# Moving the memory operands, the output rows and three buffers in a fused hybrid-trunk layer

## The chip, the cores and the metric

The kernel runs on one core of a Trainium2 chip. The metric is device time in microseconds for one execution of the whole layer: lower is better. The engines are named as in the profile: PE is TensorE (PEld its weight loads), DVE is VectorE, ACT is ScalarE, POOL is GpSimd, SP is SyncE, which here only starts DMAs.

## The reference

The layer has three residual parts on a sequence of 1024 tokens with 1024 channels, all in float32. Only the first two are touched by the change.

```python
# 1. token mixing
h = rms_norm(x, mix_pre_g)
proj = h @ w_in                                   # u | q | k | v | forget gate
y_ssm = s5_mixer(u, ...)                          # diagonal state space, GELU, GLU
y_fox = forgetting_attention(q, k, v, f_logit)    # 8 causal heads of 64
y_mix = concatenate([rms_norm(y_ssm, ssm_out_g), rms_norm(y_fox, fox_out_g)], axis=-1)
x = x + rms_norm(y_mix @ w_out, mix_post_g)
# 2. cross-attention into 256 memory tokens, 4 heads of 256
h = rms_norm(x, xa_pre_g)
x = x + rms_norm(memory_cross_attention(h, mem_n, xa_wq, xa_wkv, xa_wo), xa_post_g)
# 3. SwiGLU feed-forward
x = x + rms_norm(swiglu(h, w_gate, w_up, w_down), ffn_post_g)
```

The end of `s5_mixer` is the gated linear unit, the GLU: `g = gelu(y); out = g * sigmoid(g @ glu_w + glu_b)`. `mem_n` is `rms_norm(mem, mem_g)`, and `kv = mem_n @ xa_wkv` gives keys and values of the memory.

## The kernel before

**Arithmetic.** Every large product is made of three: an operand is split into a high part that the matmul takes as is, and a low part that is the rest (`split`, lines 113 to 117: one ScalarE pass, then one VectorE pass). `mm3` (lines 122 to 124) issues high x high, high x low and low x high.

**Order.** The kernel is one straight program without loops on the chip. A planner orders the instructions of each engine before the program runs, from a model of their times: what stands earlier in the Python text (or in a `tc.high_priority` block) goes first among those that it holds to be ready, and an instruction which needs a buffer can be placed only when one is to be had. `tc.issue_after(ins)` queues what its block holds behind `ins`; `behind()` (line 694) is that with the newest entry of the list `last`, which holds ScalarE instructions: one Gelu of the state space output, then the exponential of every attention unit.

**Buffers.** All large tiles come from a few pools. `slab`: 16 buffers of 8 KB per partition, used by nearly all stages. `raw`: two buffers of 4 KB, the landing place of most weights (`load_w`, line 152). `whl`: three buffers for split weights. The pool `t4` has tags: a (2 buffers), b (2), c (3), d (1), e (1), t2 (3), yt (2). `load_w(..., stage="e")` lands a weight in a buffer of that tag instead of in `raw`.

**The stages around the change**, with the time at which they run in the profiled execution:

- `in_proj` (up to about 230 us): the input projection, with the state space model beside it. At its end `ssm_out` (line 634) makes the state space output in two halves `s_` of four PSUM banks each, `b` 0 to 3, each ended by a Gelu (line 645), turns it (line 655) and splits it into the slabs `gl`. Two of the eight v tiles of `v1` are left over for the next stage.
- Attention, `fox` (line 696; about 228 to 486 us). A unit is one head and one block of 128 tokens, 64 in all; `scores` runs two units ahead of `turn` (transposes of the probabilities, line 758) and `values` (line 772). A score bank is freed by the VectorE pass of line 737. `prepare(h)` loads a head's queries, keys and gates on SP; `load_v(c)` loads the values of four heads. `values` collects squares in a tile of tag d.
- `fillers` (line 975) are pieces of other work that `paced` deals out beside the attention units, 1.02 for each: the rest of `v1`, the eight pieces of `glu`, the first output rows, `mem_load` (the memory, normalised and split into two slabs, its VectorE multiply at line 959), the 16 tiles of `mem_tile` (keys and values of the memory, stored to kv_d), the remaining output rows, and the first half of `build_a` (query weights times memory keys).
- `out_ssm` (line 818) makes the output rows: the state space half of the output projection, scaled by `r_s` (line 836), stored to `t1_d` on POOL's queue (line 840; the profile calls it t_d). `r_s` comes from `glu_stats`, which sums the GLU's squares, collected in `acc` (tag d), over channels (line 237). Before, it stood inside `out_ssm`, after the first two rows.
- After attention the attention half of the output projection is added. Its weights `wo` are loaded and split (lines 1024 to 1029). Then comes one loop turn `n` for each 128 tokens (line 1033): a tile `t` (tag a or b) is loaded with the half result from `t1_d` (line 1039), the matmuls' result is added (line 1046), its square is summed (line 1048), it is scaled on POOL (line 1050) and added to x (line 1054). `build_a(1)` is stepped in between.
- Then the cross-attention's output weights are folded into the memory's values (`VW`, line 1208), with eight weights `a["wo"]`, two of them landed in tag e.

## Time and profile before

| what | value |
|---|---|
| three runs | 1410.9, 1415.4, 1419.39 us; median 1415.4 |
| profiled execution | 1412.18 us |
| its span, first to last instruction | 1410.4 us |
| mean granted clock of TensorE | 0.99 |
| DMA traffic | 239.45 MB, mean 170 GB/s |

The page cuts the span into 40 slices of 35.3 us. Its rows for TensorE and its clock read:

```profile
PE   9999999999999898999999999999999999999997
PEclk9999999889999999999999999999999999999999
```

A digit is the busy share in tenths, 9 meaning 90% or more. In the second row, a digit is the clock that was granted. Slices 8 and 9 (247 to 317 us) have a lower clock, and slices 14 and 16 (458 to 494 and 529 to 564 us) a lower share. What follows looks into those places with finer stretches.

### The profile page before, as it was taken

To read this page: it belongs to the slowest core of one execution; us is meant where nothing else is said; L and a number is where in the kernel's file an instruction comes from. 1 tells how busy PE (TensorE), PEld (TensorE's weight loads), DVE (VectorE), ACT (ScalarE), POOL (GpSimd) and SP (SyncE) were. 2 spreads that over 40 slices of the span, in tenths; PEclk is the share of its full clock that TensorE was granted. 3 is DMA by queue.
4 is the path that set the end of the run, shared out by engine and by line. 5 is a ranking of instruction groups with operands and counts; after the bars stand their busy time and mean duration, and the time that the engine had idled before them with its cause. 6 is when DMAs were issued, how large, how long until landed. Compare 5 with 4: busy or idle time off the path is not lost.

```text
span 1410.4 us, 20272 instructions
## 1 busy us (share of the span) xinstructions
PE 1381.5 (98%) x7353; PEld 1163.3 (82%) x7353; DVE 952.1 (68%) x1719; ACT 652.8 (46%) x1289; POOL 378.7 (27%) x430
## 2 busy tenths in 40 slices
PE   9999999999999898999999999999999999999997
PEld 7889888889888786888888788888888888888886
DVE  8949945857666687545467767777776676555566
ACT  7383345666566555433344532333333334544351
POOL 0011110011111133001021377676766651000021
PEclk9999999889999999999999999999999999999999
DMA  6335665357562855024467345554444447965544
GB/s 217 91 107 162 204 224 135 91 165 224 187 180 95 214 185 201 1 83 159 147 213 250 102 174 195 186 173 168 144 159 151 162 150 244 344 203 194 179 165 164
DMA packets 104502, 239.45 MB, mean 170 GB/s; under 512 B 11465, under 2 KB 40137, under 8 KB 104273
## 3 DMA queue, kind: packets, MB, share of 16 engines
q1 hardware_dynamic: 85872, 176.24, 39.8%
q0 software_dynamic: 18528, 61.91, 12.3%
q8 instruction: 58, 0.95, 0.3%
q14 instruction: 44, 0.35, 0.1%
HBM read 169.43 MB, written 77.33 MB: 175 GB/s over the span
## 4 chain that ended last, share of the span: by engine, by line
PE 60%; DVE 1%; ACT 0%; issue 0%; DVEq 0%; ACTq 0%
PE x L1281 17%; PE g L1281 13%; PE x L1544 7%; PE g L1544 7%; PE x L123 2%; PE x L124 2%; PE g L122 2%; PE x L122 2%; PE g L124 2%; PE g L123 2%; PE g L1066 1%; PE g L1177 1%; DVE c L1054 0%; DVE whl L115 0%; ACT yt L1048 0%
## 5 line engine op out<-in xcount | busy, mean ns | idle before, releaser
L1281 PE MATMUL x<-slab,op 128*128 128x512 f32 x984 | 233.2, 389 | 0.5 <-DVE op L115 0.5
L1281 PEld LDWEIGHTS x<-slab,op 128*128 128x128 f32 x984 | 184.7, 188 | 39.2 <-DVE op L115 1.0
L1281 PE MATMUL g<-slab,op 128*128 128x512 f32 x744 | 178.7, 389 | 0.0
L115 DVE TENSOR_TENSOR slab<-slab 128x1024 fp32r<-128x1024 f32 (+2 forms) x92 | 110.6, 1208 | 86.6 <-ACT slab L113 84.4
L1281 PEld LDWEIGHTS g<-slab,op 128*128 128x128 f32 x744 | 139.7, 188 | 29.0
L122 PE MATMUL g<-slab,whl 128*128 128x512 f32 (+1 forms) x416 | 151.7, 365 | 0.8 <-ACT slab L485 0.4
L124 PE MATMUL g<-slab,whl 128*128 128x512 f32 (+1 forms) x416 | 148.9, 359 | 0.0
L123 PE MATMUL g<-slab,whl 128*128 128x512 f32 (+1 forms) x416 | 148.3, 356 | 0.0
L113 ACT ACTIVATE slab<-slab 128x1024 fp32r<-128x1024 f32 (+2 forms) x92 | 94.9, 1036 | 107.9 <-DMA slab<-hs_d 79.0
L1544 PE MATMUL g<-slab 128*128 128x512 f32 x462 | 126.6, 389 | 0.0
L1544 PE MATMUL x<-slab 128*128 128x512 f32 x462 | 126.6, 389 | 0.0
L1544 PEld LDWEIGHTS g<-slab 128*128 128x128 f32 x462 | 86.7, 188 | 18.0
L1544 PEld LDWEIGHTS x<-slab 128*128 128x128 f32 x462 | 86.7, 188 | 18.0
L115 DVE TENSOR_TENSOR op<-slab,op 128x512 fp32r<-128x512 f32 x80 | 84.4, 1066 | 11.6 <-ACT op L113 11.3
L1357 POOL TENSOR_TENSOR wt<-wt 128x256 f32<-128x256 f32 x88 | 83.0, 943 | 21.3 <-DMA wt<-in_w_down 18.0
L122 PEld LDWEIGHTS g<-slab,whl 128*128 128x128 f32 x416 | 78.6, 189 | 12.0 <-ACT whl L113 0.6
L124 PEld LDWEIGHTS g<-slab,whl 128*128 128x128 f32 x416 | 78.4, 189 | 11.7 <-DVE whl L115 0.2
L122 PE MATMUL g<-whl,slab 128*128 128x256 f32 (+2 forms) x288 | 86.8, 310 | 1.2 <-ACT yt L318 0.7
L123 PEld LDWEIGHTS g<-slab,whl 128*128 128x128 f32 x416 | 78.6, 189 | 10.8
L113 ACT ACTIVATE op<-slab 128x512 fp32r<-128x512 f32 x80 | 50.0, 627 | 79.3 <-PE x L1281 38.0
L124 PE MATMUL g<-whl,slab 128*128 128x256 f32 (+2 forms) x288 | 85.9, 299 | 0.0
L123 PE MATMUL g<-whl,slab 128*128 128x256 f32 (+2 forms) x288 | 85.9, 298 | 0.0
(385 smaller groups left out, 2890.6 us busy)
## 6 DMA issues: line engine op xcount, KB each, us to landing
hs_d<-ev POOLq DMA_DIRECT2D x77, 256.0 KB, 2.6
slab<-hs_d SPq DMA_DIRECT2D x35, 512.0 KB
wt<-in_w_down SPq DMA_DIRECT2D x44, 256.0 KB
wt_d<-wt POOLq DMA_DIRECT2D x22, 512.0 KB, 5.1
slab<-in_w_gate SPq DMA_DIRECT2D x20, 512.0 KB
slab<-in_w_up SPq DMA_DIRECT2D x20, 512.0 KB
slab<-wt_d SPq DMA_DIRECT2D x20, 512.0 KB
wd_d<-in_w_down SPq DMA_DIRECT2D x33, 256.0 KB
```

The lines of the kernel that those rows point to most:

```text
L113: first = act.activation(out=hi, in_=src, func=AF.Copy, scale=1.0 if mul is None else mul)
L115: (lo_eng or dve).tensor_tensor(out=lo, in0=src, in1=hi.bitcast(F32), op=ALU.subtract)
L122: pe.matmul(ps, lh, rh, start=first, stop=False)
L123: pe.matmul(ps, lh, rl, start=False, stop=False)
L124: pe.matmul(ps, ll, rh, start=False, stop=last)
L1066: pe.transpose(tp[:, k], src[:, (k0 + k) * P:(k0 + k + 1) * P], ident)
L1177: turned = pe.transpose(tp[:, k], h3[:, (4 * n + k) * P:(4 * n + k + 1) * P], ident)
L1281: pe.matmul(ps, x[:, k], y[:, k], start=first and k + n == 0, stop=k == 3 and n == 2, skip_group_check=not first)
L1357: pool.tensor_tensor(out=o, in0=x, in1=y, op=ALU.subtract)
L1544: pe.matmul(banks[n][j], xo[:, u, js], wo[:, v], start=ends[0] and k == 0, stop=ends[1] and k == 2, skip_group_check=onto is not None)
```

## The change

The diff, whole but for unchanged lines:

```diff
 def ssm_out():
-                    if (s_, b) == (0, 3):
+                    if (s_, b) == (0, 0):
                         last.append(g_)
 def glu(ys):
-        acc = tt("d")
+        acc = tt("e")
 def prepare(h):
-            sp.dma_start(out=ncb, in_=nc_d[h:h + 1, :].broadcast_to([P, S]))
             heads[h] = (qs, ka, ncb)
             q, k = qs.bitcast(F32), ka.bitcast(F32)
-            for t in range(2):
-                sp.dma_start(out=q[t * 64:t * 64 + 64], in_=qk_d[h // 2, t, r0:r0 + 64])
-            for rr in (0, 64):
-                sp.dma_start(out=k[rr:rr + 64], in_=qk_d[4 + h // 2, :, r0:r0 + 64].rearrange("t p s -> p t s"))
+            with behind():
+                sp.dma_start(out=ncb, in_=nc_d[h:h + 1, :].broadcast_to([P, S]))
+                for t in range(2):
+                    sp.dma_start(out=q[t * 64:t * 64 + 64], in_=qk_d[h // 2, t, r0:r0 + 64])
+                for rr in (0, 64):
+                    sp.dma_start(out=k[rr:rr + 64], in_=qk_d[4 + h // 2, :, r0:r0 + 64].rearrange("t p s -> p t s"))
 def fox(yf):
         prepare(0)
-        load_v(0)
...
-                if (h, t) == (3, 5):
-                    load_v(1)
+                if (h, t) in ((0, 3), (3, 5)):
+                    load_v(h // 2)
 def out_ssm(ys):
-                made = []
                 for j in range(j0, j0 + 2):
...
-                    made.append((j, ps))
-                    if cc + j0 == 0:
-                        yield
-                        if j == 0:
-                            continue
-                        glu_stats()
-                    for jj, ps in made:
-                        act.activation(out=o[:, jj - j0], in_=ps, func=AF.Copy, scale=r_s[:, jj:jj + 1])
-                    made = []
+                    act.activation(out=o[:, j - j0], in_=ps, func=AF.Copy, scale=r_s[:, j:j + 1])
                     if j == j0:
                         yield
+    mem = []
+
+    def mem_load(r):
+        rb = row_bcast(r, 2)
+        mem.extend((slab([P, KT, 256]), slab([P, KT, 256])))
+        for k in range(0, KT, 4):
+            m = raw([P, 4, 256])
+            sp.dma_start(out=m, in_=a["memT"].rearrange("(k p) m -> p k m", p=P)[:, k:k + 4])
+            for kk in range(4):
+                dve.tensor_tensor(out=m[:, kk], in0=m[:, kk], in1=rb, op=ALU.mult)
+                split(mem[0][:, k + kk], mem[1][:, k + kk], m[:, kk], g_mem[:, k + kk:k + kk + 1])
 def in_proj():
         drain(go)
+        mem_load(r_mem[0])
-    def mem_load(r, out):
...
-                with behind():
-                    dve.tensor_tensor(out=m[:, kk], in0=m[:, kk], in1=rb, op=ALU.mult)
-                    split(mh[:, k + kk], ml[:, k + kk], m[:, kk], g_mem[:, k + kk:k + kk + 1])
-                if kk % 2:
-                    yield
-        out.extend((mh, ml))
 def fillers():
         yield from glu(ys)
-        mem = []
-        rows = out_ssm(ys)
-        step(rows)
-        yield
-        for _ in mem_load(r_mem[0], mem):
-            step(rows)
-            yield
         for i in range(16):
             mem_tile(i, *mem)
+            if i == 1:
+                glu_stats()
             yield
+        rows = out_ssm(ys)
         yield from rows
         yield from build_a(0)
 # after attention
     for i in range(4):
-        w = raw([P, D])
-        sp.dma_start(out=w, in_=a["w_out_f"][i])
+        if i % 2 == 0:
+            w = slab([P, 2, D], F32)
+        sp.dma_start(out=w[:, i % 2], in_=a["w_out_f"][i])
         hl = slab([P, 2, D])
-        split(hl[:, 0], hl[:, 1], w)
+        split(hl[:, 0], hl[:, 1], w[:, i % 2])
-        t = tt("aab"[n % 3])
+        t = tt("aabaabae"[n])
 # folding wo into the memory's values
-        wo_ = [load_w(a["wo"][2 * h + d], 512, stage="e" if (2 * h + d) % 3 == 2 else None) for d in range(2)]
+        wo_ = [load_w(a["wo"][2 * h + d], 512, stage={2: "a", 5: "e"}.get(2 * h + d)) for d in range(2)]
```

In words:

- The memory's operands are made at the end of `in_proj`, right behind `ssm_out`, in the order of the text and no longer behind an attention unit. Before, they were made in four pieces among the fillers after the GLU.
- `glu_stats` follows the second memory tile, and all output rows come after the sixteenth.
- The GLU's sum of squares `acc` lies in tag e instead of d.
- The loads of `prepare` stand in a `behind()` block, the list `last` begins with an earlier Gelu, and the first half of the values is loaded at unit (0, 3) instead of ahead of the loop.
- The attention half of the output projection's weights lands in two slabs instead of in `raw`.
- In the loop after attention, the last tile `t` (n = 7) has tag e instead of a. The third weight folded into the memory's values (number 2) lands in tag a instead of e; the sixth (number 5) stays in e.

## The prediction

> **What bounds the kernel now.** I read the page first (span, engines, chain), then tables of busy time by stretch, then the waits of TensorE, then the timeline of the stretches in which it has gaps.

> ```profile
> span 1410.4 us, 20272 instructions
> PE 1381.5 (98%) x7353; PEld 1163.3 (82%) x7353; DVE 952.1 (68%) x1719; ACT 652.8 (46%) x1289; POOL 378.7 (27%) x430
> ```

> TensorE has something in flight for all but 28.9 us. The diff adds or drops no matmul, so it can only win TensorE's gaps and the time in which its clock is held down. The table by stretch (columns: stretch and length, then busy time of PE, PEld, DVE, ACT, POOL, then granted clock, DMA share, GB/s) shows where these lie in the part that the diff touches:

> ```profile
> 270.30:273.30 3.00, 1.04 (x11) 0.63 (x10) 3.00 (x9) 2.97 (x6) 0.00 (x0) 0.94 0.00 0
> 273.30:290.00 16.70, 14.20 (x59) 11.95 (x61) 11.29 (x27) 11.33 (x26) 1.31 (x2) 0.50 0.47 133
> 464.00:493.00 29.00, 24.81 (x176) 19.77 (x175) 16.72 (x28) 14.61 (x28) 2.85 (x3) 1.00 0.83 221
> 535.00:537.00 2.00, 1.08 (x5) 0.80 (x5) 1.77 (x7) 1.41 (x6) 1.41 (x1) 1.00 0.65 203
> 547.10:552.90 5.80, 3.46 (x13) 1.91 (x11) 3.07 (x6) 2.34 (x11) 2.19 (x2) 0.99 0.28 93
> 552.90:559.50 6.60, 5.33 (x12) 3.77 (x13) 6.46 (x9) 6.55 (x11) 0.57 (x1) 0.50 0.47 159
> ```

> A matmul at clock 0.50 takes twice its time, so half of the busy time at 0.50 is lost beside the gaps.
> Stretch A (270.3 to 290.0): gaps 1.96 + 2.50, clock 14.20 / 2 = 7.10; together 11.6 us.
> Stretch B (547.1 to 559.5): gaps 2.34 + 1.27, clock 5.33 / 2 = 2.67; 6.3 us.
> Stretch C (464 to 493): gaps of 4.2 us at full clock.
> With 0.9 at 535, that is 23.0 us, the most that the change can win here.

> [...]

> **Stretch A: why it stops, and what the change does.** VectorE is busy 3.00 of the 3.00 us in which TensorE starves:

> ```profile
> 272.31 0.95 DVE L737 CUSTOM_DVE_ANT_0 c<-s,b 128x768 f32<-128x768 f32 x1
> 273.33 0.80 PE L730 MATMUL s<-slab,a 128*128 128x512 f32 x1 [2.00 <-DVE nlr L737]
> ACT d L782 <- PE g L237: 1.8, 1, 1.8
> 282.21 1.06 ACT L113 ACTIVATE whl<-raw 128x1024 fp32r<-128x1024 f32 x1 [2.95 <-DMA raw<-in_wkv]
> 284.20 0.82 ACT L836 ACTIVATE t<-g,r_s 128x256 f32<-128x256 f32 x2
> PE g L758 <- ACT t L836: 2.2, 1, 2.2
> L959 DVE TENSOR_TENSOR raw<-raw,t 128x256 f32<-128x256 f32 x8 | 2.8, 420 | 0.0
> L117 DVE SCALAR_TENSOR_TENSOR slab<-raw,gains,slab 128x256 fp32r<-128x256 f32 x8 | 3.5, 480 | 0.0
> L113 ACT ACTIVATE slab<-raw,gains 128x256 fp32r<-128x256 f32 x8 | 3.6, 501 | 0.0
> ```

> Four things meet. The score pass L737, which frees a score bank, queues on VectorE behind the memory operands (8 x 0.42 + 8 x 0.48, listed as 2.8 and 3.5 us busy). The square of the first value block (L782) needs tag d, which the GLU's sum holds until the token sums L237. The memory projection's weights come late, because the raw buffers hold the memory itself. And the first output rows keep PSUM banks until r_s exists (L836), so a transpose waits 2.2 us.

> Each has its edit. The memory operands move to the end of in_proj, where the engines are free:

> ```profile
> 200.00:225.00 25.00, 24.69 (x211) 24.46 (x212) 5.06 (x8) 11.22 (x21) 2.16 (x4) 1.00 0.52 138
> L645 ACT ACTIVATE slab<-g x8: 592/598/616, 199.6 to 217.2; 128x512 f32<-128x512 f32 x8
> ```

> VectorE has 19.9 us free there and ScalarE 13.8, against the 6.3 and 3.6 us that move. So they cost nothing while that cover holds; without it they cost at most their 6.3. The acc tile goes to tag e, so L782 waits for nothing of the GLU. The rows go last, long after r_s. What is late next: the third memory weight wants tag e, so its load must wait for the token sums after memory tile 1. A memory weight's fetch, ScalarE and VectorE passes bound that: nothing if the planner runs tile 3 first, 2.95 us (the ScalarE wait above) if not; I take 2. Behind this load on SP stand the weight of tile 3, inside the same bound, and the next head's keys, which are wanted a head later: 0. With about 1 us of crowding at L737 left, A gives 8.5 of its 11.6.

> **The price at the front.** The two memT loads (two DMAs on SP) are now traced ahead of the GLU weights and share two raw buffers with them:

> ```profile
> L665 SPq DMA_DIRECT2D raw<-in_glu_w x2: 328/330/333, 168.0 to 179.7; - x2
> 227.33 1.06 ACT L113 ACTIVATE whl<-raw 128x1024 fp32r<-128x1024 f32 x1 [0.91 <-PE g L124]
> 232.94 0.48 PE L122 MATMUL g<-slab,whl 128*128 128x512 f32 x1
> ```

> Now the GLU weights are fetched at 168 and 180 and used at 233. They will leave SP only when the memory operands are written, and these need two slabs. All 16 slabs are taken until the first half of the state space output ends (8 of xs, 2 each of U, T, SS, mo); its Gelus start at 199.6, so I expect both slabs soon after 200 and the GLU weights by about 215. Cost 0; bounds 0 and 5 (rival 3); I take 1. Later the slabs just suffice: at the GLU's last matmuls gl 4, ys 3, memory 2, keys 2, values 1 and probabilities 4 make 16. load_v(0) six steps later only asks for its slab later; 0. It moves one 1 MB DMA past prepare(1)'s on SP; the first values are due at unit (1,1), six units on, so nobody waits.

> The block around prepare's five loads on SP names a ScalarE instruction; as I read issue_after, it binds only instructions of that same engine, so it does nothing here, and nor does the earlier Gelu in last. Cost 0; if it did bind, SP would hold the next head's loads and all behind them, with the 2.0 us of the longest L730 wait as nearest price.

> The rows' move takes six of their pieces, with three of the stores on POOL, behind the memory tiles and their kv_d stores:

> ```profile
> L840 POOL DMA_DIRECT2D t_d<-t x16: 715/725/732, 285.3 to 451.5; - x16
> L1039 SPq DMA_DIRECT2D b<-t_d x4: 574/596/642, 455.6 to 463.8; - x4
> ```

> The last store stays build_a's eight pieces ahead of the end, and its readers begin 4.1 us behind it now, with TensorE full; 0, at worst that 4.1. POOL's first store no longer waits for r_s. Fillers: 67 pieces become 66 for the 68 that the rate asks for; one piece less cover at the end costs between 0 and the largest gap of A, 2.2 us; I take 0.5.

> **Stretch C.** The out-projection weights shared raw with the query weights:

> ```profile
> 475.97 1.06 ACT L113 ACTIVATE slab<-raw 128x1024 fp32r<-128x1024 f32 x1 [5.05 <-DMA raw<-in_w_out_f]
> 477.08 0.73 PE L122 MATMUL x<-slab 128*128 128x512 f32 x2 [1.55 <-ACT slab L113]
> ```

> ScalarE stood 5.05 us for that load, TensorE 1.55. Two slabs, each filled by two DMAs, cut the tie to raw, but six slabs must now come free at the end of attention instead of four. So a slab's wait may replace the raw buffer's: between -4.2 (all gaps gone) and +4.2 (as many again); I take -1.

> **Stretch B.** The last half result takes the freed buffer a:

> ```profile
> 538.03 0.58 SPq L1039 DMA_DIRECT2D a<-t_d  x1
> 539.88 0.58 SPq L1039 DMA_DIRECT2D a<-t_d  x1
> 548.27 0.75 DVE L1046 SCALAR_TENSOR_TENSOR a<-x,r_f,a 128x512 f32<-128x512 f32 x1 [2.33 <-DMA a<-t_d]
> 549.05 0.42 ACT L1048 ACTIVATE yt<-a 128x256 f32<-128x256 f32 x1 [3.74 <-DVE a L1046]
> 552.78 1.04 ACT L113 ACTIVATE whl<-raw 128x1024 fp32r<-128x1024 f32 x1
> 553.88 2.08 PE L122 MATMUL x<-whl,b 128*128 128x512 f32 x4 [1.74 <-ACT whl L113]
> 526.23 0.38 SPq L158 DMA_DIRECT2D e<-in_wo  x1
> L124 PE MATMUL g<-e,whl x48: 274/283/283, 451.8 to 518.5; 128*128 128x256 f32 x48
> DMA to landing us min/median/max: 2.5/3.2/9.6
> 547.10 0.39 PE L122 MATMUL x<-whl,b 128*128 128x512 f32 x1
> 554.97 1.22 DVE L115 TENSOR_TENSOR whl<-raw,whl 128x1024 fp32r<-128x1024 f32 x1
> ```

> The load starts at 538, lands at 548; L1046, the squares and the next weight split queue behind it. Tag e is free after 518.5, so in the changed kernel the data are there some 20 us early. In exchange the third output weight of the memory stage moves from e (issued at 526.2) to a, free only at 538; with the 2.5 to 9.6 us to landing of the t_d transfers and passes of 1.04 and 1.22 it is ready between 543 and 550, and it is wanted at 547: 0 to 3 us. Behind it on SP stand the last x tile and the sixth weight, wanted after 549. VectorE is busy 6.46 of 6.60 us after 552.9, and idle 2.73 of 5.80 before, so it can take back some 3 to 5 us of work, not more. I take 4.5 of the 6.3, which includes that.

> **Sum.** -8.5 (A) + 1 (GLU weights) + 0.5 (fillers) - 1 (C) - 4.5 (B) = -12.5 us. The profiled execution took 1412.2 us (span 1410.4 and 1.8 around it), which gives 1399.7. The median of the three runs, 1415.4, is 3.2 above it; so I forecast 1403 for the median.

> **Rivals.**
> 1. The memory operands are not made beside the state space output: the planner gets no slabs for them before attention begins, and their 6.3 us of VectorE meet the first scores instead. For it: the slabs are full until 199.6. Against it: VectorE's 19.9 free us. A's gain shrinks to about 1; total -5: 1410. Chance 0.22, no change.
> 2. B's gain is lost: the third weight in a lands at 548 and the e buffer gives the sixth late. Total -8: 1407. Chance 0.14, of which 0.09 below the bound.
> 3. Slower: the raw buffers. If the two slabs come only after 229, when the last v tile frees xs, the GLU weights leave SP there; as the weights issued at 276.64 were split at 282.21, they need 5.6 us, then 2.3 for the split: first GLU matmul at 237.6, 4.7 later than now, the second weight 2.3 behind. TensorE has only the first head's short scores, and falls to 0.50 as in A, 7.1 more; A's own gap comes back at the third memory weight. -5.5 + 4.7 + 2.3 + 7.1 = +8.6: 1424. It decides once the slabs come later than about 222. Chance 0.13.

> ```profile
> 276.64 8.24 SPq L158 DMA_DIRECT2D raw<-in_wkv  x2
> ```

> **How the numbers follow.** Half a per cent (7.1 us) is about what a measurement of this kernel can tell from no change: 1408.3 and 1422.5 are the bounds. Forecast 0.46 (1398 to 1408); all 23 us won, 1392, 0.05; rivals 0.22, 0.14, 0.13. Faster 0.46 + 0.05 + 0.09 = 0.60; same 0.22 + 0.05 = 0.27; slower 0.13. The range 1390 to 1419 leaves out rival 3 and a little below.

> **What would show it.** Right: L959 before 225 and done in two raw buffers before the GLU weights' loads; TensorE's clock at 1.00 from 262 to 290; no wait of TensorE on L836; L782 without a wait on L237; no VectorE wait on the t_d load of the last tile. Wrong: a clock of 0.50 anywhere between 185 and 290, the GLU's first matmul after about 235, a TensorE wait on a weight split of memory tile 2, or a ScalarE wait on in_wo near 545. A planner that reorders the late stages throughout would break the forecast in a way that no row here prices.

## The result, and the profile after

The changed kernel takes **1420.1 us** (median of 20 runs, 1417.2 to 1424.9) beside 1414.5 for the kernel before in the same measurement (1410.9 to 1419.4). The ratio is 1.0043, with a 95% interval of 1.0032 to 1.0054: slower by 0.43%, some 6 us. The forecast was 1403 with a range of 1390 to 1419, so the direction was wrong and the median lies 1.1 us above the range.

The page of the changed kernel, its span and its engines (busy time, share of the span, instructions):

```profile
span 1421.5 us, 20274 instructions
PE 1383.1 (97%) x7353; PEld 1163.4 (82%) x7353; DVE 947.2 (67%) x1719; ACT 653.4 (46%) x1289; POOL 377.5 (27%) x430
```

TensorE has 38.4 us without work in flight (1421.5 - 1383.1), before 28.9: its work is the same, its gaps are not. One caution: this execution took 1423.3 us, 3.2 above its median, and the one profiled before (1412.2) lay 2.3 below its own. So half of the 11.1 us between the two spans is the place of two executions in their spread, and what a stretch costs is settled further down by medians.

The table by stretch shows where the time lies (length, busy time of PE, PEld, DVE, ACT and POOL, granted clock, DMA share, GB/s). Before:

```profile
175.00:250.00 75.00, 71.44 (x498) 64.84 (x497) 39.94 (x69) 40.23 (x71) 7.53 (x14) 1.00 0.56 169
250.00:300.00 50.00, 45.54 (x284) 38.52 (x284) 36.10 (x88) 35.62 (x78) 2.00 (x3) 0.83 0.50 132
450.00:525.00 75.00, 70.81 (x467) 59.92 (x466) 54.84 (x104) 43.10 (x107) 16.31 (x15) 1.00 0.66 188
525.00:575.00 50.00, 45.48 (x192) 35.61 (x191) 39.96 (x75) 32.34 (x86) 15.59 (x11) 0.93 0.49 166
```

After:

```profile
175.00:250.00 75.00, 68.54 (x464) 62.52 (x463) 38.47 (x71) 35.94 (x65) 7.53 (x14) 0.95 0.60 168
250.00:300.00 50.00, 42.69 (x267) 36.64 (x266) 37.98 (x76) 35.67 (x68) 1.63 (x3) 0.90 0.46 133
450.00:525.00 75.00, 67.41 (x450) 56.42 (x448) 52.59 (x109) 44.99 (x109) 14.81 (x14) 0.95 0.65 173
525.00:575.00 50.00, 45.86 (x204) 37.07 (x203) 36.09 (x63) 26.68 (x78) 17.04 (x13) 0.93 0.60 199
```

A stretch's loss is its length less PE's busy time, plus busy time x (1 - clock). The second term is an estimate that takes a matmul at clock 0.50 for twice its time: in the kernel before, four 128x512 matmuls in a row take 2.08 us at 0.50 (from 553.88) and 1.07 at full clock (from 561.57), 1.94 times. By that, before and after: the front (175 to 250) 3.6 and 9.9; stretch A (250 to 300) 12.2 and 11.6; C (450 to 525) 4.2 and 11.0; B (525 to 575) 7.7 and 7.4. So A and B, where 13 us were to be won, kept their size, and the front and C lost 6 to 7 more each. The four differences add up to 12.2, close to the 11.1 of the spans.

**The front.** The timeline of the changed kernel on SP, VectorE, ScalarE and TensorE (start, duration, engine, line, output and input, idle time before it and what ended it). L867 and L869 are the memory's load and multiply, L175 the copy that ends `row_bcast`, L665 the GLU weights:

```profile
169.15 12.09 SPq L867 DMA_DIRECT2D raw<-in_memT  x2
226.32 2.48 DVE L115 TENSOR_TENSOR slab<-g,slab 128x512 fp32r<-128x512 f32 x4 [12.47 <-ACT slab L113]
227.61 0.42 ACT L175 ACTIVATE t<-g 128x256 f32<-128x256 f32 x1
228.72 2.76 DVE L869 TENSOR_TENSOR raw<-raw,t 128x256 f32<-128x256 f32 x8
233.09 1.92 SPq L665 DMA_DIRECT2D raw<-in_glu_w  x2
240.11 0.50 PE L122 MATMUL g<-slab,whl 128*128 128x512 f32 x1 [0.82 <-ACT whl L113]
```

The memory waits in both raw buffers from 169 to 229. VectorE stands idle for 12.47 us just before it gets to it, since the pass ahead in its queue (L115, the last split of the state space output) waits for ScalarE. The row by which the memory is multiplied was not there sooner either: its copy L175 ends at 228.0, behind the same splits on ScalarE. The GLU weights leave SP at 233 instead of 168 and 180, and the first GLU matmul starts at 240.1 instead of 232.9.

Not all of these 7.2 us belong to the GLU weights. The state space output ends late too: its last matmuls start at 221.1 instead of 216.8. The first of them had waited longer, as the two timelines show (before, then after; L643 makes the state space output, L632 loads its operand from T_d):

```profile
188.77 0.46 PE L643 MATMUL g<-slab 128*128 128x128 f32 x2 [0.96 <-DMA slab<-T_d]
191.50 0.46 PE L643 MATMUL g<-slab 128*128 128x128 f32 x2 [2.74 <-DVE a L115]
```

Behind the longer wait the clock was at 0.50 for 3.4 us (192.8 to 196.2). From the last of these matmuls to the first of the GLU it takes 19.0 us instead of 16.2, so 2.8 of the 7.2 us come behind the state space output, and the other 4.4 ahead of its end.

**Stretch A.** The same view around the third memory weight, and TensorE's longest wait there:

```profile
283.37 1.05 PE L237 MATMUL g<-ones,e 128*128 128x1 f32 x8
284.60 7.63 SPq L158 DMA_DIRECT2D e<-in_wkv  x2
289.55 1.06 ACT L113 ACTIVATE whl<-e 128x1024 fp32r<-128x1024 f32 x1 [4.00 <-DMA e<-in_wkv]
290.66 0.58 PE L122 MATMUL g<-slab,whl 128*128 128x256 f32 x1 [6.24 <-ACT whl L113]
```

All the old waits of this stretch are gone (L836's rows, tag d, most of the score pass's). In their place stands one: the token sums read tag e until 284.42, the weight's load leaves SP 0.2 us later, and TensorE waits 6.24 us for it.

**Stretch B.** The last half result is in e now. SP and VectorE, in order of time (L1022 loads an x tile, L1025 a half result, L1032 adds the matmuls' result to it, L1040 adds a finished tile to x):

```profile
531.63 4.84 SPq L1022 DMA_DIRECT2D c<-in_x  x2
536.56 1.23 SPq L1025 DMA_DIRECT2D e<-t_d  x2
537.03 1.28 DVE L1040 SCALAR_TENSOR_TENSOR c<-a,r,c 128x1024 f32<-128x1024 f32 x1
538.38 1.22 SPq L1025 DMA_DIRECT2D a<-t_d  x2
551.15 0.75 DVE L1032 SCALAR_TENSOR_TENSOR a<-x,r_f,a 128x512 f32<-128x512 f32 x1 [5.15 <-DMA a<-t_d]
558.29 0.74 DVE L1032 SCALAR_TENSOR_TENSOR e<-x,r_f,e 128x512 f32<-128x512 f32 x1
```

The load into e stands in SP's queue behind x tiles. What those wait for is in SP's own waits from 500 to 560 (total, times, longest):

```profile
SPq L1022 <- DMA x_d<-c: 19.2, 5, 9.2
```

An x tile's buffer comes free only when the store of an earlier tile has landed. So the half result in e leaves at 536.6, though tag e was last read at 530.9 (L124). It is in time even so: its add at 558.29 waits for nothing. The one before it, in a, is late now, by 5.15 us. Its load leaves at 538.38, right after L1040 has read its buffer for the last time (537.03 + 1.28), and its add starts 12.8 us later. In the kernel before, the load of this tile left at 530.64, its add started 9.8 us later, and the wait was 0.40.

**Stretch C.** The out-projection weights through slabs:

```profile
476.73 0.90 SPq L1012 DMA_DIRECT2D slab<-in_w_out_f  x2
487.08 1.06 ACT L113 ACTIVATE slab<-slab 128x1024 fp32r<-128x1024 f32 x1 [4.27 <-DMA slab<-in_w_out_f]
488.18 2.08 PE L122 MATMUL x<-slab 128*128 128x512 f32 x4 [3.87 <-ACT slab L113]
```

The first of them leaves SP at 476.7 and is split 10.4 us later; TensorE waits 3.87 us and then runs at clock 0.50 (a 128x512 matmul takes 0.63 us there and starts 0.43 after the one ahead of it; at full clock, from 493.6 on, it is 0.39 and 0.23).

### The profile page after: what moved, and what is told of

The parts are those of the page before. It is cut to its first block, busy times and chain, and to the rows that moved or that the text cites. A ratio compares the mean times of both kernels' runs of the same rounds, so it can differ in the third digit from the quotient of the medians.

```text
span 1421.5 us, 20274 instructions
## 1 busy us (share of the span) xinstructions
PE 1383.1 (97%) x7353; PEld 1163.4 (82%) x7353; DVE 947.2 (67%) x1719; ACT 653.4 (46%) x1289; POOL 377.5 (27%) x430
## 4 chain that ended last, share of the span: by engine, by line
PE 59%; DMA 2%; DVE 1%; ACT 0%; issue 0%; POOL 0%; SPq 0%; DVEq 0%; POOLq 0%
PE x L1267 17%; PE g L1267 13%; PE x L1530 7%; PE g L1530 7%; PE x L123 2%; PE x L124 2%; PE g L122 2%; PE x L122 2%; PE g L124 2%; PE g L123 2%; PE g L1052 1%; DMA a<-t_d 1%; DMA x_d<-c 1%; PE g L1163 1%; DMA a<-in_wo 0%; DVE c L1040 0%
## 5 line engine op out<-in xcount | busy, mean ns | idle before, releaser
L115 DVE TENSOR_TENSOR slab<-slab 128x1024 fp32r<-128x1024 f32 (+2 forms) x96 | 115.2, 1208 | 97.7 <-ACT slab L113 96.0
L122 PE MATMUL g<-slab,whl 128*128 128x512 f32 (+1 forms) x416 | 152.6, 367 | 7.9 <-ACT whl L113 7.5
L113 ACT ACTIVATE slab<-slab 128x1024 fp32r<-128x1024 f32 (+2 forms) x96 | 99.1, 1038 | 117.2 <-DMA slab<-hs_d 80.4
L124 PE MATMUL g<-slab,whl 128*128 128x512 f32 (+1 forms) x416 | 148.4, 359 | 0.0
L122 PEld LDWEIGHTS g<-slab,whl 128*128 128x128 f32 x416 | 79.5, 191 | 19.3 <-ACT whl L113 7.9
L115 DVE TENSOR_TENSOR op<-slab,op 128x512 fp32r<-128x512 f32 x80 | 86.6, 1093 | 11.7 <-ACT op L113 11.4
L124 PEld LDWEIGHTS g<-slab,whl 128*128 128x128 f32 x416 | 78.9, 190 | 11.5 <-DVE whl L115 0.2
L113 ACT ACTIVATE op<-slab 128x512 fp32r<-128x512 f32 x80 | 50.0, 628 | 82.9 <-PE g L1267 40.6
L123 PEld LDWEIGHTS g<-slab,whl 128*128 128x128 f32 x416 | 79.4, 191 | 10.5
L122 PE MATMUL g<-whl,slab 128*128 128x256 f32 (+2 forms) x288 | 85.5, 305 | 1.7 <-ACT yt L318 0.7
L123 PE MATMUL g<-whl,slab 128*128 128x256 f32 (+2 forms) x288 | 85.1, 295 | 0.0
L124 PE MATMUL g<-whl,slab 128*128 128x256 f32 (+2 forms) x288 | 84.9, 295 | 0.0
```

The lines of the kernel that those rows point to most:

```text
L113: first = act.activation(out=hi, in_=src, func=AF.Copy, scale=1.0 if mul is None else mul)
L115: (lo_eng or dve).tensor_tensor(out=lo, in0=src, in1=hi.bitcast(F32), op=ALU.subtract)
L122: pe.matmul(ps, lh, rh, start=first, stop=False)
L123: pe.matmul(ps, lh, rl, start=False, stop=False)
L124: pe.matmul(ps, ll, rh, start=False, stop=last)
```

## The experiments

All are edits of the changed kernel, and every time was taken beside the kernel before on the same chip (there 1412.6 to 1413.9 us; the experiments were spread over four chips, so kernels are compared by their ratios). The table gives the medians; "loss" is worked out for the four stretches as above.

| kernel | median, us | ratio to before (95%) | front | A | C | B |
|---|---|---|---|---|---|---|
| before | 1414.5 | 1 | 3.6 | 12.2 | 4.2 | 7.7 |
| changed | 1420.1 | 1.0043 (1.0032 to 1.0054) | 9.9 | 11.6 | 11.0 | 7.4 |
| e1 operands earlier | 1413.4 | 1.0003 (0.9995 to 1.0012) | 7.1 | 7.4 | 7.8 | 7.5 |
| e2 memory not in raw | 1412.9 | 0.9995 (0.9987 to 1.0004) | 4.4 | 7.2 | 7.7 | 8.4 |
| e3 third weight not in e | 1414.8 | 1.0012 (1.0001 to 1.0024) | 11.8 | 8.0 | 7.4 | 7.6 |
| e4 slabs undone | 1420.3 | 1.0057 (1.0044 to 1.0070) | 5.7 | 11.8 | 10.1 | 7.4 |
| e5 e2 and e3 together | 1404.8 | 0.9946 (0.9928 to 0.9965) | 5.5 | 0.0 | 7.6 | 6.8 |
| e6 e5, slabs undone | 1407.9 | 0.9960 (0.9946 to 0.9975) | 4.8 | 0.2 | 5.8 | 8.2 |
| e7 e5, last half result undone | 1404.9 | 0.9940 (0.9922 to 0.9958) | 5.6 | 0.2 | 9.8 | 5.0 |
| e8 e5, rows in the middle | 1410.1 | 0.9978 (0.9967 to 0.9989) | 5.5 | 0.1 | 9.6 | 6.6 |
| e9 e1 and e3 together | 1406.1 | 0.9958 (0.9944 to 0.9971) | 6.8 | 0.0 | 7.6 | 7.4 |
| e10 e5, rate 0.98 | 1414.7 | 1.0014 (0.9998 to 1.0029) | 7.5 | 1.9 | 11.5 | 8.8 |
| e11 e2, sum back on d | 1406.0 | 0.9957 (0.9944 to 0.9969) | 4.5 | 0.0 | 8.0 | 7.1 |
| e12 e5, rate 1.06 | 1412.7 | 0.9995 (0.9983 to 1.0006) | 4.9 | 0.0 | 16.6 | 6.7 |

The losses come from one execution each: e3 and e4 run the changed kernel's program up to stretch A and lose 11.8 and 5.7 us in the front where it lost 9.9. So a loss is good to about 3 us, and a verdict rests on the ratios.

### e1: the same buffers, an earlier time

```diff
             step(v1, n)
             step(go)
+            if n == 2:
+                mem_load(r_mem[0])
         drain(go)
-        mem_load(r_mem[0])
```

> The changed kernel with one call moved: the memory operands are traced after the first half of the state space output instead of after the whole of it, so that the multiplies and splits stand between the first and the second four Gelus in the queues of VectorE and ScalarE. The raw buffers stay the ones used. Theory (the raw buffers): in the changed kernel the GLU weights left SP at 233.1 only because both raw buffers held the memory until its multiplies at 228.7, which are last in the queues; with the multiplies near 200 both GLU weights leave SP before 220, the first GLU matmul comes at about 233 instead of near 240, and 5 to 7 us go: 1413 to 1415. The wait of 6.2 us on the third memory weight stays. Rival (slabs): the splits wait for slabs that come free only after 225, so the order of the queues does not matter: GLU weights still at about 233, 1419 to 1421. Rival (the state space output itself is late, by its T slabs): also no change.

Measured: 1.0003, 6 us below the changed kernel (0.0040 x 1414). The source view of the multiplies and of the GLU weights (count, then minimum, median and maximum in ns, then the first and last start):

```profile
L869 DVE TENSOR_TENSOR raw<-raw,t x8: 418/419/425, 205.4 to 207.7; 128x256 f32<-128x256 f32 x8
L665 SPq DMA_DIRECT2D raw<-in_glu_w x2: 338/338/339, 209.7 to 212.5; - x2
```

The multiplies start at 205, some twenty microseconds sooner, the splits into the slabs at 206, and the GLU weights leave 2 us behind the last multiply. So two slabs can be had at 205 in this order. In the changed kernel itself the first split, at 229.16, waits for the multiply and for no slab. What kept the operands until 229 was their place in the queues. The first GLU matmul came at 237.6, not at the 233 that the theory gave, since the state space output ends late here as it does in the changed kernel (last start of L643 at 221.4, before at 216.6). From its end to the GLU it takes 16 us again, as before the change. So the second rival, a late state space output, holds for that part of the delay.

### e2: the same time, other buffers

```diff
-            m = raw([P, 4, 256])
+            m = tt("ed"[k // 4], [P, 4, 256])
```

> The changed kernel, with the two halves of the memory landing in tags e and d instead of the two raw buffers; when the operands are made is left as it is. Theory (the raw buffers): the GLU weights are fetched near 170 to 180 as before the change, and the GLU starts at about 233 although the multiplies still run at 228: 5 to 7 us go, 1413 to 1415. Rival (crowding): what delays the GLU is that the multiplies and splits of the memory sit ahead of the GLU weight splits on ScalarE and VectorE; then the GLU weights arrive early, but at most 2 us go: 1418 to 1420.

Measured: 0.9995, 7 us below the changed kernel. The multiplies still run at 224 to 227, and the GLU weights:

```profile
L665 SPq DMA_DIRECT2D raw<-in_glu_w x2: 328/331/334, 168.0 to 179.7; - x2
```

They leave at the times of the kernel before, and the first GLU matmul is at 234.3. The state space output is in time too, with its last matmuls at 216.8. Two cures that share the earlier release of the raw buffers give nearly the same 6 to 7 us; in their traces a third to a half of it lies in the front (9.9 to 7.1 and to 4.4), the rest in A and C. The rival, crowding of the splits on ScalarE and VectorE, allowed 2 and falls.

The wait ahead of the first L643 goes with the memory in raw. In the five kernels that have it there (the changed one, e1, e3, e4, e9) it is 2.0 to 3.4 us, and in all but e4 the clock falls (its mean from 175 to 200 is 0.93, 0.93, 0.86, 1.00 and 0.93). In eight others (all but e12, for which the wait is not shown) it is 1.0 to 1.7 us, with a mean clock of 1.00. In e3, e4 and e9 the profile names the T_d load as what ended it. Why that load lands later with the memory in raw is not shown.

### e3: the third memory weight

```diff
-        wh, wl = load_w(a["wkv"][i], P, stage="e" if i % 3 == 2 else None)
+        wh, wl = load_w(a["wkv"][i], P, stage="e" if i % 3 == 2 and i > 2 else None)
```

> The changed kernel, with the weight of memory tile 2 alone through a raw buffer instead of tag e; the weights of tiles 5, 8, 11 and 14 stay on e. Theory (tag e): in the changed kernel this weight leaves SP at 284.6, because the GLU's running sum holds e until the token sums, and TensorE waits 6.2 us and then runs at clock 0.50; without the tie the wait goes, and with it most of the 6.2 us and of the time at half clock: 7 to 11 us faster, 1409 to 1413, with a clock of 0.9 or more from 280 to 300. Rival (no room on raw): the weight waits for a raw buffer instead, as the memory weights did before the change with 2.95 us of ScalarE; 0 to 4 us faster, and the clock still falls.

Measured: 1.0012, 4 us below the changed kernel by the ratios (5.3 by the medians), less than the theory's 7 to 11. The wait of 6.2 us is gone, but smaller ones came up. ScalarE's waits from 250 to 300:

```profile
ACT t L960 <- DMA kv_d<-t: 3.6, 1, 3.6
ACT whl L113 <- DMA raw<-in_wkv: 3.2, 2, 1.6
```

This is nearer to the rival's 0 to 4, and the clock still falls (0.69 from 290 to 295). With the weight on raw, the next thing late is a memory tile's output buffer, whose store has not landed, and then the weight fetches themselves.

### e4: the slabs of the out-projection weights

```diff
-        if i % 2 == 0:
-            w = slab([P, 2, D], F32)
-        sp.dma_start(out=w[:, i % 2], in_=a["w_out_f"][i])
+        w = raw([P, D])
+        sp.dma_start(out=w, in_=a["w_out_f"][i])
         hl = slab([P, 2, D])
-        split(hl[:, 0], hl[:, 1], w[:, i % 2])
+        split(hl[:, 0], hl[:, 1], w)
```

> The changed kernel, with the out-projection weights back through the raw buffers, one load and one buffer each, as before the change; nothing else undone. Theory (slabs): their loads in the changed kernel come late because six slabs have to come free at the end of attention instead of four, and the stretch from 450 to 525 loses 10.5 us instead of 4.2; the undoing gives back about 6 us: 1413 to 1415, with the weight splits some 15 us earlier. Rival: the stretch is longer because the output rows and their stores now stand at the end of attention, beside the same loads, and the slabs are not the cause: 0 to 2 us, 1418 to 1420.

Measured: 1.0057, not below the changed kernel, and C still loses 10.1. The slabs are not what C's loss hangs on; the theory falls. The first weights do come earlier, but then the third one stops ScalarE, and the attention's last copy (L764) queues behind its split:

```profile
486.67 1.06 ACT L113 ACTIVATE slab<-raw 128x1024 fp32r<-128x1024 f32 x1 [7.75 <-DMA raw<-in_w_out_f]
489.48 1.12 PE L773 MATMUL g<-slab 128*64 128x256 f32 x4 [3.10 <-ACT slab L764]
```

### e5: both mended

The edits of e2 and e3.

> The changed kernel with the second and the third experiment together: the memory lands in tags e and d, and memory tile 2's weight goes through raw. Alone they took off 7.2 and 5.3 us of the changed kernel's 1420.1. Theory (two separate buffer waits): they add, 1407 to 1409, with no clock of 0.50 between 175 and 300. Rival (the second loss is partly an echo of the first: with the front mended the third memory weight's wait is already 4.0 instead of 6.2 us, and with its weight on raw ScalarE waits for the outputs of the memory tiles): 1410 to 1412, and some loss stays in 275 to 300.

Measured: **1404.8 us**, ratio 0.9946 (0.9928 to 0.9965), faster than both kernels: 8 to 9 us below before, 14 to 15 below the changed kernel. The two cures at least add up (6.8 + 4.4 = 11.2 us by the ratios, 13.7 together); the 2.5 us beyond the sum are within the intervals. The table of the four stretches:

```profile
175.00:250.00 75.00, 69.52 (x488) 63.19 (x487) 43.67 (x81) 42.38 (x77) 7.53 (x14) 1.00 0.58 176
250.00:300.00 50.00, 50.00 (x369) 44.14 (x369) 38.49 (x82) 38.55 (x78) 3.37 (x7) 1.00 0.65 179
450.00:525.00 75.00, 68.82 (x422) 57.12 (x418) 53.70 (x100) 41.97 (x112) 21.70 (x19) 0.98 0.70 203
525.00:575.00 50.00, 46.45 (x198) 37.04 (x197) 34.25 (x62) 27.14 (x67) 8.54 (x7) 0.93 0.29 105
```

Stretch A has no loss at all: TensorE is busy 50.00 of 50 us at full clock, where it lost 12.2 before. So the change did hold what it was forecast to win there, and more; two choices of a buffer had hidden it.

### e6, e7, e8: the other parts, with the front mended

e6 adds the edit of e4 to e5.

> The fifth experiment's kernel, and the out-projection weights back through raw, one load and one buffer each. With the front mended the end of attention lies where it lay before the change. Theory (slabs): the slabs' loads put the first weight split some 7 us later than before the change; undone, the stretch from 450 to 525 loses about 4 us again instead of 8: 3 to 4 us faster than the fifth experiment. Rival (the DMA engines, which are full there, set the landing whatever the buffer; as in the fourth experiment): within 1 us of the fifth.

Measured: 0.9960 beside 0.9946, 2 to 3 us slower than with slabs, with intervals that overlap. Neither theory is borne out as it stood: the slabs show no cost, if anything they win a little. In the trace C loses 5.8 instead of 7.6 and B 8.2 instead of 6.8, both within the 3 us to which a loss is good.

e7 undoes stretch B's part in e5:

```diff
-        t = tt("aabaabae"[n])
+        t = tt("aab"[n % 3])
...
-        wo_ = [load_w(a["wo"][2 * h + d], 512, stage={2: "a", 5: "e"}.get(2 * h + d)) for d in range(2)]
+        wo_ = [load_w(a["wo"][2 * h + d], 512, stage="e" if (2 * h + d) % 3 == 2 else None) for d in range(2)]
```

> The fifth experiment's kernel, with the last half result back on tag a and the third and sixth output weights of the memory stage back on e. Theory (the wait only changed its place: in the changed kernel the loads stand on SP behind an x tile, whose buffer waits for the store of an earlier tile, so both the load in e and the one in a leave at 536 to 538): within 1 us of the fifth. Rival (the buffer of its own does win the 4.5 us that were forecast, hidden by losses ahead of it): 3 to 5 us slower than the fifth.

Measured: 1404.9 beside 1404.8 us. The part wins nothing, as the theory had it. In e5 SP has the same order as in the changed kernel, and again the half result in a leaves when its buffer comes free (L1040 ends at 520.19) and is waited for:

```profile
518.41 1.23 SPq L1025 DMA_DIRECT2D e<-t_d  x2
520.22 1.22 SPq L1025 DMA_DIRECT2D a<-t_d  x2
532.46 0.75 DVE L1032 SCALAR_TENSOR_TENSOR a<-x,r_f,a 128x512 f32<-128x512 f32 x1 [4.31 <-DMA a<-t_d]
```

With the part undone it is the last tile's half result that is waited for, 2.85 us:

```profile
543.40 0.75 DVE L1032 SCALAR_TENSOR_TENSOR a<-x,r_f,a 128x512 f32<-128x512 f32 x1 [2.85 <-DMA a<-t_d]
```

e8 puts the output rows of e5 between memory tiles 7 and 8:

```diff
             yield
-        rows = out_ssm(ys)
-        yield from rows
+            if i == 7:
+                yield from out_ssm(ys)
```

> The fifth experiment's kernel, with the output rows after memory tile 7 instead of after tile 15; they still come after r_s. Theory (the rows at the end crowd the loads of the out-projection weights and the half results): 2 to 4 us faster than the fifth, lost in the stretch from 450 to 525. Rival (the rows' place costs nothing once r_s exists): within 1 us.

Measured: 0.9978, 4 to 5 us slower than e5, with intervals that don't overlap. Both theories miss: the place of the rows matters, and last is the better of these two places. That the rows crowd the end of attention gets no support.

### e9, e11: the other cure of each clash

e9 joins e1 and e3: raw keeps the memory, but not so long.

> The first and the third experiment together: the memory stays in the raw buffers, but its operands are made after the first half of the state space output, and memory tile 2's weight goes through raw. It mends the same two waits as the fifth experiment (1404.8 us) by other edits: the one by time instead of by buffer. Theory (it is the hold of the raw buffers that counts): 1404 to 1407, TensorE without a clock of 0.50 between 175 and 300, and GLU weights leaving SP before 222. Rival (the fifth's gain hangs on tags e and d, or on the operands being made late, beside the first scores): 1409 or more.

Measured: 1406.1 us, 0.9958: within the theory's numbers, though the clock did dip in the front (a mean of 0.93 from 175 to 200; the front loses 6.8). The gain does not hang on tags e and d.

e11 takes e2 and puts the GLU's sum back on tag d, so that the third weight may stay on e:

```diff
-        acc = tt("e")
+        acc = tt("d")
```

> The second experiment's kernel with the GLU's running sum back on tag d, as before the change; memory tile 2's weight is on e as in the changed kernel, where nothing holds it now. It is the other cure of that clash: not the weight is moved but the sum. Theory (two users of one tag are the whole clash, and the wait for d was the smaller one, 1.8 us of ScalarE in the first value block): 1404 to 1408. Rival (the sum on d brings the old gap of the first scores back, 12 us in the stretch from 250 to 300): 1411 to 1416.

Measured: 1406.0 us, 0.9957, and no loss in A. Beside e2 (0.9995) that is 5 us by ratios, 7 by medians, from one letter. The move of the sum to e wins nothing here: the wait for d that it was to end costs TensorE nothing once the memory operands and the rows are out of the way.

### e10, e12: the rate of the side pieces

```diff
-RATE = 1.02
+RATE = 0.98
```

> The fifth experiment's kernel with the rate of the side pieces at 0.98 instead of 1.02 per step of attention, so that the 66 pieces last about three steps longer. In the fifth, TensorE's gaps between 450 and 475 are 5.7 us, against 1.6 before the change. Theory (the pieces run out and leave the last units of attention uncovered): 2 to 4 us faster than the fifth, 1401 to 1403. Rival (those gaps come from the loads and splits of the out-projection weights): within 1 us, or up to 3 us slower, because the last pieces then stand beside the out projection.

e12 is the same line at 1.06:

> The fifth experiment's kernel (1404.8 us) with the rate of the side pieces at 1.06, so that the 66 pieces are done in 63 steps of attention instead of 65. At 0.98 it lost 10 us: the out-projection weights were split late (TensorE waited 7.1 us) and waits came back at 225 to 350. Theory (the side pieces hold the raw buffers, slabs and DMA engines that the end of attention needs, so earlier is better): 1399 to 1404, with less than 7 us lost between 450 and 500. Rival (the rate of 1.02 is the place where units of attention and pieces just cover each other, and any shift uncovers some): 1406 or more.

Measured: 1414.7 and 1412.7 us, 7 to 10 slower than e5. The rate of 1.02 fits and these two don't; in e12 the rival's number is right, in e10 neither expected so much. At 0.98 all four stretches lose 2 to 4 us more than in e5, at 1.06 only C does (9.0). TensorE's waits from 445 to 530 have one large entry each, the first split of an out-projection weight. At 0.98:

```profile
PE x L122 <- ACT slab L113: 7.1, 1, 7.1
```

At 1.06:

```profile
PE x L122 <- ACT slab L113: 9.2, 1, 9.2
```

In e5 this wait is 2.3 us. In both, ScalarE itself stands waiting for that weight's load, 8.4 and 12.1 us.

## Why the prediction was wrong

**The price at the front** is the step whose mending wins most. It read: "I expect both slabs soon after 200 and the GLU weights by about 215. Cost 0; bounds 0 and 5 (rival 3); I take 1." They left at 233, and mending that alone is worth 6 to 7 us (e1, e2). The argument had added up VectorE's free time in 200 to 225 (19.9 us) and called it cover. But the memory's passes stood behind those of the state space output, in the queues of TensorE, ScalarE and VectorE: 12.47 us of the free time lay ahead of the pass in front of them, and the row they multiply by was copied only at 228.0. Placed sooner in the text, the same passes ran from 205 on (e1). Here free time was cover only for what came next in the queue and had its inputs.

A second part of this price had no term at all: with the memory in raw, TensorE waits longer ahead of the state space output (2.74 us instead of 0.96) and then runs at clock 0.50 for 3.4 us, which makes up most of the 4.4 us that the state space output is late. Rival 3 had the consequence right (raw buffers held, weights late, a gap at the third memory weight; +8.6 forecast, +5.6 measured by the medians), but named another cause, late slabs; in the changed kernel the splits wait for the multiplies, and e1 splits at 206. It got 0.13.

**Stretch A** was forecast at 8.5 of 11.6, and the changed kernel won almost nothing there. The mechanism was right: the score pass, the rows and the old wait went, and with the buffers mended the whole 12.2 is won (e5, e9, e11). What failed is the term "nothing if the planner runs tile 3 first, 2.95 us if not; I take 2". The price was taken from a ScalarE wait on raw, which has two buffers; tag e has one, and is read until the token sums are over. A full load, from issue at 284.60 to the split at 289.55, then stands on TensorE's path: 6.24 us, and a clock of 0.50 behind it until 295.2. Nor was anything gained for it: with the sum back on d, A loses nothing (e11). The wait for d was a row of the profile, but a row that others covered.

**Stretch B** was forecast at 4.5 and gave nothing (e7). The failing step is the working from one tile: "in the changed kernel the data are there some 20 us early". For the last tile that came true in effect: its load leaves 21.7 us ahead of its add, which waits for nothing. But the tile before it is still in a, and the wait of 2.33 us came back there as 5.15: its load leaves when its buffer comes free, and the data come after the engines want them. What the neighbour in a would then wait for had no term. Why that load takes 12.8 us to its add instead of 9.8 is not shown.

**Stretch C** was put at -1 between -4.2 and +4.2. The trace of the changed kernel shows +6.8, and +3.2 to +3.6 in e1, e2 and e3, whose text is the same there. By e4 and e6 the slabs don't carry it. What does is open. In e5 the first weight, issued at 461.2, is split at 470.4; in e12 one issued at 465.5 is split at 478.2, with the DMA engines full in both (share 1.02 from 466 to 471 in e5, 1.00 to 1.05 from 466 to 478 in e12). That the loads queued around it set its landing is argued, not shown.

**The small terms.** 0.5 for one piece less among the fillers could not be seen by itself; a shift of the rate by 4% costs 7 to 10 us (e10, e12), so the balance of pieces and attention units is far sharper than the largest gap of A, from which the bound was taken. The block around `prepare`'s loads and the earlier Gelu do nothing, as forecast: with both undone, all five engines get the same instructions in the same order. The move of `load_v` was not tried by itself.

**The sum.** As terms of e5's trace against before, where only the two buffers differ from the change: front +1.9 (forecast +1), A -12.2 (-8.5), C +3.4 (-1), B -0.9 (-4.5). That is -7.8, and the spans differ by 7.6. Each of these four is good to about 3 us only, and only A is well clear of that. The forecast of 12.5 for the change missed by some 18 us on the medians, and two choices of a buffer are 14 to 15 of these (e5). Of the signs that the prediction named, three for wrong came (a clock of 0.50 between 185 and 290, the first GLU matmul after 235, a wait of TensorE on the split of memory tile 2), and so did three for right (no wait on the output rows' copies, none of the first square on the token sums, none on the last tile's half result).

## What to carry to other kernels

Before a buffer gets a second user, write down its holder's last read and the queue in which the next load stands; idle time on an engine proves nothing if the pass ahead in its queue, or an input, comes late (here 12.47 us of VectorE's). When one tile of a loop gets a buffer of its own, look at its neighbours: the wait can move to them. A part that gains can be hidden by a neighbour that loses: undo suspicious parts alone and together before the change is dropped, since here neither cure alone beat the kernel before and the two together did by 0.5%. A wait in the profile is worth removing only if nothing else ends at the same time: with the sum back on d, whose wait was 1.8 us of ScalarE's before, A loses 0.0 (e11).

## What was new about the hardware

Three gaps cost more than themselves, and not in proportion to their length. In the changed kernel TensorE stopped at 284.42 and began again at 290.66; its clock (the last figure but two), by microsecond:

```profile
285.00:286.00 1.00, 0.00 (x0) 0.00 (x0) 0.35 (x3) 0.51 (x2) 0.00 (x0) 0.50 0.84 258
295.00:296.00 1.00, 1.00 (x10) 1.00 (x9) 0.54 (x2) 0.43 (x1) 0.00 (x0) 0.90 0.74 274
```

It fell within 0.6 us of the last matmul and came back 4.5 us after the first. In e1, with a gap from 279.94 to 284.12, it fell only at the gap's end and came back 6.5 us after the first matmul:

```profile
283.00:284.00 1.00, 0.00 (x0) 0.00 (x0) 0.00 (x0) 0.99 (x2) 0.00 (x0) 0.91 0.92 238
290.00:291.00 1.00, 1.00 (x7) 1.00 (x7) 0.69 (x1) 0.04 (x1) 0.00 (x0) 0.67 0.79 315
```

In e12, after the long wait that ended at 479.28, it took 3.3 us:

```profile
482.00:483.00 1.00, 1.00 (x8) 0.53 (x7) 0.28 (x1) 0.00 (x0) 0.87 (x1) 0.73 0.51 205
```

```profile
276.33:279.75 3.42, 3.16 (x16) 3.08 (x16) 2.53 (x9) 1.38 (x4) 0.00 (x0) 0.50 0.88 194
286.57:289.99 3.42, 3.42 (x17) 2.38 (x18) 2.40 (x6) 3.42 (x8) 0.59 (x1) 0.50 0.79 259
```

A piece with TensorE busy for 3.16 of 3.42 us did not bring the clock back, nor did the two that follow it, busy for 2.75 and 1.86; the last, busy throughout for 3.42, did. In e12 the last piece ahead of the rise, 479.13 to 482.54, begins 0.15 us before the first matmul, so TensorE was busy for 3.26 us of it at most, and the clock came back as well. What sets the times of fall and rise is not shown.
